# Four modulation vectors of a decoder layer: from ScalarE and GpSimd to VectorE, with new charges in a work-filling planner

## The chip, the cores and the metric

The kernel runs on one core of one Trainium2 chip. Its five engines are TensorE (PE in the profile, with PEld for its weight loads), VectorE (DVE), ScalarE (ACT), GpSimd (POOL) and SyncE (SP, which here only issues transfers). Each engine works through its own instructions in order. The metric is the device time of one execution in microseconds (us); lower is better.

## The reference, cut to what matters

One layer of a conditioned decoder for 1024 tokens of width 1024. A conditioning vector `c` gives six modulation vectors; two of them (shift 1, scale 1) are needed before anything else, the other four only later:

```
mod = silu(c) @ w_ada + b_ada          # 6 vectors of 1024: sh1, sc1, gt1, sh2, sc2, gt2
h   = rmsnorm(x, g_norm1) * (1 + sc1) + sh1
z   = h @ w_in                         # GLU pair | q | k | v | o | i | f | gate A | gate B
A   = silu(layernorm(dwconv31(glu_a * sigmoid(glu_b)))) @ w_conv_out
B   = mlstm_chunkwise(conv4(q), conv4(k), v, i, f) @ w_m_out
x   = x + gt1 * ((sigmoid(gA) * A + sigmoid(gB) * B) @ w_out)
h   = rmsnorm(x, g_norm2) * (1 + sc2) + sh2
out = rmsnorm(x + gt2 * hierarchical_moe(h), g_final)
```

## The kernel before, in words

Everything is float32. A matrix product is made of three products of rounded parts: a weight piece `raw` is split into a high part `wh` (cast on ACT, L150) and a low part `wl` (subtraction on DVE, L56), and the tokens are there as `hH` and `hL`.

The first half of the kernel is a list of PE jobs over the columns of `w_in` (`z_cols`, `z_tokens`, `z_tokens_wide`; the tiles `z` and `zt` are their sums). In order: the first GLU columns, the wide job (o columns and the i and f gates), the v columns, eight q and k jobs, two more o jobs, and sixteen jobs for the branch gates (A and B in turn, budget 7.5 each). PE works through the jobs one behind the other; the other engines' work is put between them by hand.

This is done by `fill(budget)`, called twice in a job. It takes one step of each of three queues of generators: `lat` (preparation of the mLSTM gates, then `mlstm()`, whose chunks pass through `step_a`, `step_b` and `step_c`), `lat2` (`conv_norm()`, which waits until `bulk` is empty) and `aux` (`ada_rest()`, later `clear_y()`, which writes zeros to `y_d`). What a step yields is its charge. The budget less the charges of `lat` and `lat2` is credit for `bulk`: the convolution of width 31, `conv31(m)` for four blocks of channels, one DVE operation a tap on 128x1024 elements (`cacc<-u,vec,cacc`, L64), charged 1.14. `aux` is stepped but not charged. So the tables of charges decide how many taps stand on DVE between two splits.

`ada_rest()` computes the four late vectors. Each has four blocks; a block is a transfer of 1 MB of `w_ada` into `ar` (two buffers, issued on SP behind the weight pieces `raw`) with two rows per partition. Before the change ACT multiplies each row by its element of silu(c) (L574), in place, and POOL adds it to `acc` (`tt(..., eng=G)`, L56; 28 additions in all). `column_sums` then sums `acc` over the partitions with PE (tile `modp`) and DVE writes `modc`.

When the jobs are done, `drain()` steps what is left of the queues: the mLSTM output is transposed (`psT`), scaled on ACT (`hs`, L903) and split (`bHt`, `bLt`), and the convolution result `cacc`, normed and through silu on ACT (L968), is split into `uH` (ACT) and `uL` (DVE). The first branch job (`yTrue`) needs all of `uH` and `uL`. After the branches come the product with `w_out`, routing, and the experts, whose weights fill the memory's bandwidth.

Of the kernel before, what the change touches and what calls it, by code (L numbers as in the profile page):

```python
# [12 lines left out]
AF = mybir.ActivationFunctionType  # L13
OP = mybir.AluOpType
# [4 lines left out]
P = 128  # L19
# [23 lines left out]
def hybrid_layer_kernel(ctx: ExitStack, tc: tile.TileContext, x, c, w_ada, b_ada, g_norm1, w_in, b_if,  # L43
# [9 lines left out]
    V, S, G, PE = nc.vector, nc.scalar, nc.gpsimd, nc.tensor  # L53

    def tt(o, a, b, op, eng=V):
        return eng.tensor_tensor(out=o, in0=a, in1=b, op=op)  # L56

    def ts(o, a, s1, op0, s2=None, op1=None, eng=V):
        if op1 is None:
            return eng.tensor_scalar(out=o, in0=a, scalar1=s1, scalar2=None, op0=op0)  # L60
        return eng.tensor_scalar(out=o, in0=a, scalar1=s1, scalar2=s2, op0=op0, op1=op1)

    def stt(o, a, s, b, op0, op1):
        return V.scalar_tensor_tensor(out=o, in0=a, scalar=s, in1=b, op0=op0, op1=op1)  # L64

    def mm(o, l, r, start, stop):
        return PE.matmul(o, l, r, start=start, stop=stop)  # L67
# [27 lines left out]
    silc = cst.tile([P, KT], F32, name="silc")  # L95
# [42 lines left out]
    def adab(vi, j, n):  # L138
        return vec[:, 64 + vi * KT + j:64 + vi * KT + j + n]
# [140 lines left out]
    lat, lat2, bulk, aux = [], [], [], []  # L280

    def step(q):
        while q:
            try:
                return next(q[0])
            except StopIteration:
                q.pop(0)
        return 0

    credit = [0.0]  # L290

    def fill(budget):

        credit[0] += budget - step(lat) - step(lat2)
        step(aux)
        while credit[0] > 0.5 and bulk:
            credit[0] -= step(bulk)
        if not bulk:
            credit[0] = 0.0
# [175 lines left out]
    def z_cols(c0, n, use, budget):  # L475

        W.add(w_in_k[:, :, c0:c0 + n], [P, KT, n])

        def job():
            wh, wl = W.take()  # L480
            ps = zps.tile([P, 2, 512], F32, tag="z", name=f"z{c0}")
            for k in range(KT):
                for j, (a, b) in enumerate(((wh, hH), (wh, hL), (wl, hH))):
                    for hf in range(2):
                        mm(ps[:n, hf, :], a[:, k, :], b[:, k, hf * 512:(hf + 1) * 512],
                           k == 0 and j == 0, k == KT - 1 and j == 2)
                if k == KT // 2 - 1:
                    fill(budget / 2)
            use(ps[:n].rearrange("p a b -> p (a b)"))
            fill(budget / 2)  # L490
        jobs.append(job)
# [55 lines left out]
    def ada_rest():  # L547
        raws = {}

        def load(i):  # L550
            vi = REST[i // 4]
            raws[i] = uo.tile([P, 2, D], F32, tag="ar", bufs=2, name=f"ar{i}")
            k = 2 * (i % 4)
            nc.sync.dma_start(raws[i], ada_v[:, k:k + 2, vi * D:(vi + 1) * D])

        def column_sums(n, acc):
            ps = mps.tile([P, 512], F32, tag="m", name=f"modp{n}")
            for j in range(KT):
                mm(ps[:, j:j + 1], acc[:, j * P:(j + 1) * P], ones[:, 0:1], True, True)
            tt(modc[:, n, :], ps[:, 0:KT], adab(REST[n], 0, KT), OP.add)  # L560

        load(0)
        yield 0
        pend = None
        for n in range(4):
            if pend:
                column_sums(*pend)
            acc = ml.tile([P, D], F32, tag="acc", bufs=1, name=f"acc{n}")
            for i in range(4 * n, 4 * n + 4):
                if i + 1 < 16:  # L570
                    load(i + 1)
                k = 2 * (i % 4)
                for q in range(2):
                    S.activation(raws[i][:, q, :], raws[i][:, q, :], AF.Copy, scale=silc[:, k + q:k + q + 1])  # L574
                if i % 4 == 0:
                    tt(acc, raws[i][:, 0, :], raws[i][:, 1, :], OP.add, eng=G)
                else:
                    for q in range(2):
                        tt(acc, acc, raws[i][:, q, :], OP.add, eng=G)
                yield 0  # L580
                yield 0
            pend = (n, acc)
        yield 0
        yield 0
        column_sums(*pend)
        yield 0
        yield 0
        yield 0
        ps = mps.tile([P, 512], F32, tag="m", name="modt")
        PE.transpose(ps[0:32, 0:P], modc.rearrange("p a b -> p (a b)"), ident)  # L590
        row = ml.tile([32, P], F32, name="modrow")
        S.copy(row, ps[0:32, 0:P])
        S.dma_start(mod_d[:, :], row)
# [181 lines left out]
    def hb(ap):  # L775
        return ap.unsqueeze(2).broadcast_to([P, NH, P])

    def mlstm():
# [30 lines left out]
        def step_b(cc):  # L809
            sl = slice(cc * P, (cc + 1) * P)  # L810
            PT, kw = held.pop(cc)
            vt = vts.pop(cc)
            psB = mps.tile([P, 3, P + 1], F32, tag="m", name=f"psB{cc}")

            def parts(i, name):
                t_ = mps.tile([P, 3, P + 1], F32, tag="m", name=f"{name}{cc}")
                return [t_[:, h, :] for h in range(3)] + [psB[:, i, :]]

            if cc > 0:
                psI = parts(0, "psI")  # L820
                for h in range(NH):
                    mm(psI[h], qT[h][:, sl], Cst[:, h, :], True, True)
            psN = parts(1, "psN")
            for h in range(NH):
                mm(psN[h], PT[:, h, :], vt[:, h, :], True, True)
            if cc + 1 < NT:
                psC = parts(2, "psC")
                for h in range(NH):
                    mm(psC[h], kw[:, h, :], vt[:, h, :], True, True)
                for h in range(NH):  # L830
                    if cc == 0:
                        V.tensor_copy(Cst[:, h, :], psC[h])
                    else:
                        stt(Cst[:, h, :], Cst[:, h, :], scl[:, cc, h:h + 1], psC[h], OP.mult, OP.add)
            num = ml.tile([P, NH, P + 1], F32, tag="num", name=f"num{cc}")
            den = ml.tile([P, NH], F32, tag="den", bufs=2, name=f"den{cc}")
            for h in range(NH):
                if cc > 0:
                    S.activation(num[:, h, :], psI[h], AF.Copy, scale=sint[:, cc, h:h + 1])
                    tt(num[:, h, :], num[:, h, :], psN[h], OP.add)  # L840
                else:
                    V.tensor_copy(num[:, h, :], psN[h])
            yield 4.0
            load_v(cc + 1)
            sos[cc] = ml.tile([P, NH, P], F32, tag="so", name=f"so{cc}")
            nc.sync.dma_start(sos[cc].rearrange("p h d -> p (h d)"), so_d[cc])
            hm = WT[cc]
            stt(den, num[:, :, P], -1.0, num[:, :, P], OP.mult, OP.max)
            tt(den, den, flo[:, cc, :], OP.max)
            V.reciprocal(den, den)  # L850
            tt(hm, num[:, :, 0:P], hb(den), OP.mult)
            bst = ml.tile([P, NH, 6], F32, tag="bst", bufs=2, name=f"bst{cc}")
            mv = ml.tile([P, NH, 2], F32, tag="mv", bufs=2, name=f"mv{cc}")
            lv = ml.tile([P, NH], F32, tag="lv", bufs=2, name=f"lv{cc}")
            for h in range(NH):
                V.bn_stats(out=bst[:, h, :], in_=hm[:, h, :])
            for h in range(NH):
                V.bn_aggr(out=mv[:, h, :], in_=bst[:, h, :])
            ts(lv, mv[:, :, 1], LN_EPS, OP.add)
            rsqrt(lv, lv, NH)  # L860
            held["n"] = (cc, mv, lv)
# [12 lines left out]
        for cc in range(NT):  # L874
            yield from step_b(cc)
            if cc + 1 < NT:
                step_a(cc + 1)
            yield 4.5
            step_c()
        yield 1.5  # L880
        while aux:
# [96 lines left out]
    for m in range(KT):  # L978
        for c0, dst in ((C_GA, sga_d), (C_GB, sgb_d)):
            def use(ps, c0=c0, m=m, dst=dst):  # L980
                sg = e4(f"g{c0}_{m}")
                S.activation(sg, ps, AF.Sigmoid)
                G.dma_start(dst[m], sg)
                if m == 0 and c0 == C_GA:
                    lat.append(mlstm())
                if m == 1 and c0 == C_GA:
                    lat2.append(conv_norm())
            z_cols(c0 + m * P, P, use, 7.5)


    bjobs = []
# [1115 lines left out]
```

## Time and profile before

| | us |
|---|---|
| median of 3 runs (1410.01 to 1417.47) | 1415.64 |
| the profiled execution | 1420.27 |
| its span, first to last instruction | 1418.5 |
| PE busy in it | 1305.4 (92%) |
| DVE busy | 986.0 (70%) |
| ACT busy | 515.2 (36%) |
| POOL busy | 311.9 (22%) |

Busy times are of the whole span. The page also cuts the span into 40 slices of some 35.5 us, with a digit for the busy tenths of each, and the clock that TensorE was granted, in tenths of full speed. The jobs over `w_in` end at about 581 us; from about 850 us on the transfers of expert weights are busy nearly all the time.

### The profile page before, as it was taken

The numbers are of one execution on the slowest core, as the hardware profiler recorded it, in microseconds if no ns is written. First come the engines' busy times: TensorE is split into PE (matmuls) and PEld (weight loads), VectorE is DVE, ScalarE is ACT, GpSimd is POOL, SyncE is SP. The second block draws the span as 40 slices with busy tenths as digits, with TensorE's granted clock in tenths as the row PEclk, the third lists the DMA queues.
The fourth block names the chain that finished last, engine by engine and source line by source line (L and its number), as shares of the span: only waits on it lengthen the run. The fifth ranks groups of instructions, "written<-read, shape, count | busy, mean of one in ns | idle before, by whom it ended". The sixth has DMA issues, their size and how long they took to land. (4 is left out here: it accounts for less than half of the span.)

```text
span 1418.5 us, 17679 instructions
## 1 busy us (share of the span) xinstructions
PE 1305.4 (92%) x6619; PEld 975.6 (69%) x6619; DVE 986.0 (70%) x1370; ACT 515.2 (36%) x685; POOL 311.9 (22%) x258
## 2 busy tenths in 40 slices
PE   3799888999999999999999689999999999998987
PEld 3578888879878888787888555666464756564643
DVE  5979998889976752556457776357575968585636
ACT  5232243323532224411232333235353735353523
POOL 2424355240421400105232102111010211110002
PEclk9899999999999999999999799999999999999999
DMA  8432434332453443454621449899999999999996
GB/s 280 138 119 94 174 121 148 107 112 80 148 171 124 145 140 107 143 182 148 197 90 74 182 179 381 322 360 404 412 410 405 410 381 415 391 413 387 404 352 264
DMA packets 121304, 337.50 MB, mean 238 GB/s; under 512 B 12532, under 2 KB 74272, under 8 KB 96384
## 3 DMA queue, kind: packets, MB, share of 16 engines
q1 hardware_dynamic: 106064, 290.81, 55.0%
q0 software_dynamic: 14672, 43.94, 8.2%
q10 hardware_dynamic: 480, 1.59, 0.3%
q8 instruction: 53, 0.87, 0.2%
q14 instruction: 35, 0.29, 0.1%
HBM read 303.37 MB, written 41.98 MB: 243 GB/s over the span
## 5 line engine op out<-in xcount | busy, mean ns | idle before, releaser
L56 DVE TENSOR_TENSOR wl<-big,wh 128x1024 fp32r<-128x1024 f32 x184 | 224.2, 1256 | 96.1 <-ACT wh L150 95.1
L150 ACT CAST wh<-big 128x1024 fp32r<-128x1024 f32 x184 | 185.8, 1049 | 156.1 <-DMA big<-in_w_e_gate_dram 83.0
L64 DVE SCALAR_TENSOR_TENSOR cacc<-u,vec,cacc 128x1024 f32<-128x1024 f32 x120 | 211.1, 1759 | 2.9
L67 PE MATMUL z<-hH,wh 128*128 128x512 f32 x512 | 168.6, 411 | 9.7 <-DVE hH L379 7.1
L67 PE MATMUL gu<-wh,tHLx 128*128 128x512 f32 x528 | 172.5, 408 | 2.3 <-ACT wh L150 1.1
L67 PE MATMUL z<-hL,wh 128*128 128x512 f32 x512 | 162.2, 398 | 0.2 <-POOL hL L56 0.2
L67 PE MATMUL z<-hH,wl 128*128 128x512 f32 x512 | 162.4, 399 | 0.0
L67 PE MATMUL gu<-big,tFx 128*64 128x512 f32 (+1 forms) x528 | 127.1, 617 | 0.0
L67 PEld LDWEIGHTS z<-hH,wh 128*128 128x128 f32 x512 | 97.3, 194 | 32.3 <-issue 8.7
L67 PEld LDWEIGHTS gu<-wh,tHLx 128*128 128x128 f32 x528 | 98.6, 192 | 28.9 <-ACT wh L150 6.6
L67 PEld LDWEIGHTS z<-hL,wh 128*128 128x128 f32 x512 | 97.7, 191 | 24.8 <-POOL hL L56 0.7
L67 PE MATMUL gu<-wl,tHLx 128*128 128x512 f32 x264 | 108.1, 409 | 6.9 <-DVE wl L56 6.9
L67 PEld LDWEIGHTS z<-hH,wl 128*128 128x128 f32 x512 | 97.8, 191 | 23.1
L1628 POOL DMA_INDIRECT y_d<-ye,idx x24 | 37.7, 1572 | 334.8 <-DVE ye L64 313.5
L56 DVE TENSOR_TENSOR wl<-raw,wh 128x1024 fp32r<-128x1024 f32 (+1 forms) x45 | 70.6, 1573 | 41.0 <-ACT wh L150 41.0
L67 PEld LDWEIGHTS gu<-big,tFx 128*64 128x64 f32 (+1 forms) x528 | 38.8, 142 | 70.9 <-issue 69.6
L56 POOL TENSOR_TENSOR acc<-acc,ar 128x1024 f32<-128x1024 f32 x24 | 71.1, 2961 | 59.8 <-ACT ar L574 50.8
L67 PE MATMUL zt<-wl,hH 128*128 128x256 f32 (+1 forms) x256 | 74.1, 289 | 5.2 <-DVE wl L56 5.2
L67 PE MATMUL zt<-wh,hH 128*128 128x256 f32 (+1 forms) x256 | 75.3, 294 | 1.3 <-ACT ev L634 1.2
L67 PE MATMUL zt<-wh,hL 128*128 128x256 f32 (+1 forms) x256 | 74.3, 290 | 0.0
L67 PE MATMUL py<-wh,tHLh 128*128 128x512 f32 x256 | 72.6, 404 | 0.5 <-DVE tHLx L56 0.4
L67 PE MATMUL o<-woH,mHL 128*128 128x512 f32 x256 | 72.9, 400 | 0.0
(419 smaller groups left out, 2164.9 us busy)
## 6 DMA issues: line engine op xcount, KB each, us to landing
big<-in_w_e_gate_dram SPq DMA_DIRECT2D x64, 1024.0 KB, 9.5
big<-in_w_e_up_dram SPq DMA_DIRECT2D x64, 1024.0 KB
big<-in_w_e_down_dram SPq DMA_DIRECT2D x64, 1024.0 KB, 9.5
raw<-in_w_in_dram SPq DMA_DIRECT2D x38, 512.0 KB, 4.3
ar<-in_w_ada_dram SPq DMA_DIRECT2D x16, 1024.0 KB, 6.2
araw<-in_w_ada_dram SPq DMA_DIRECT2D x8, 1024.0 KB, 10.1
y_d<-zero SPq DMA_DIRECT2D x16, 512.0 KB, 5.3
xall<-in_x_dram SPq DMA_DIRECT2D x8, 512.0 KB, 9.4
```

The costliest lines, as they stand in the source:

```text
L56: return eng.tensor_tensor(out=o, in0=a, in1=b, op=op)
L64: return V.scalar_tensor_tensor(out=o, in0=a, scalar=s, in1=b, op0=op0, op1=op1)
L67: return PE.matmul(o, l, r, start=start, stop=stop)
L150: S.copy(h, src)
L1628: G.indirect_dma_start(out=y_d[:, :], out_offset=bass.IndirectOffsetOnAxis(ap=idx[:, 1:2], axis=0), in_=src, in_offset=None, bounds_check= ...
```

## The change: what it does

In `ada_rest()` the eight rows of a vector are now taken up by DVE alone: the first by one `tensor_scalar` (`acc = row * silc`), each of the other seven by one `scalar_tensor_tensor` (`acc = row * silc + acc`). The 32 multiplications on ACT and the 28 additions on POOL are gone, 32 operations on DVE are new. There is one step to an operation, so two to a block as before, and each step is charged 0.6; `fill` now takes the charge of `aux` off the credit as well. In `mlstm()` the two charges of a chunk go from 4.0 and 4.5 to 3.4 each. The branch-gate jobs get a budget of 9.0 in place of 7.5.

```diff
     def fill(budget):
 
-        credit[0] += budget - step(lat) - step(lat2)
-        step(aux)
+        credit[0] += budget - step(lat) - step(lat2) - (step(aux) or 0)
         while credit[0] > 0.5 and bulk:
             credit[0] -= step(bulk)
...
                 k = 2 * (i % 4)
                 for q in range(2):
-                    S.activation(raws[i][:, q, :], raws[i][:, q, :], AF.Copy, scale=silc[:, k + q:k + q + 1])
-                if i % 4 == 0:
-                    tt(acc, raws[i][:, 0, :], raws[i][:, 1, :], OP.add, eng=G)
-                else:
-                    for q in range(2):
-                        tt(acc, acc, raws[i][:, q, :], OP.add, eng=G)
-                yield 0
-                yield 0
+                    if k + q == 0:
+                        ts(acc, raws[i][:, q, :], silc[:, 0:1], OP.mult)
+                    else:
+                        stt(acc, raws[i][:, q, :], silc[:, k + q:k + q + 1], acc, OP.mult, OP.add)
+                    yield 0.6
             pend = (n, acc)
...
-            yield 4.0
+            yield 3.4
             load_v(cc + 1)
...
-            yield 4.5
+            yield 3.4
             step_c()
...
-            z_cols(c0 + m * P, P, use, 7.5)
+            z_cols(c0 + m * P, P, use, 9.0)
```

On DVE, around the splits of the two pieces of the wide job (`wl` from `raw` 128x1056), this stood before:

```order
L56 TENSOR_TENSOR wl_852<-raw_715,wh_851 128x1056
L64 SCALAR_TENSOR_TENSOR cacc_626<-u_618,vec,cacc_626 128x1024 x7
L56 TENSOR_TENSOR wl_922<-raw_785,wh_921 128x1056
L56 TENSOR_TENSOR modc<-modp_952,vec 128x8
L64 SCALAR_TENSOR_TENSOR cacc_626<-u_618,vec,cacc_626 128x1024
```

and this stands there now:

```order
L56 TENSOR_TENSOR wl_844<-raw_713,wh_843 128x1056
L64 SCALAR_TENSOR_TENSOR acc_672<-ar_807,silc,acc_672 128x1024
L64 SCALAR_TENSOR_TENSOR cacc_626<-u_618,vec,cacc_626 128x1024 x3
L64 SCALAR_TENSOR_TENSOR acc_672<-ar_807,silc,acc_672 128x1024
L64 SCALAR_TENSOR_TENSOR cacc_626<-u_618,vec,cacc_626 128x1024 x2
L56 TENSOR_TENSOR wl_910<-raw_780,wh_909 128x1056
L56 TENSOR_TENSOR modc<-modp_940,vec 128x8
L60 TENSOR_SCALAR acc_950<-ar_874,silc 128x1024
```

Between the two splits seven taps have become five taps and two of the new operations.

Further on, at the start of the mLSTM (`PT` and `kw` are the first chunk's, `wl` the splits of branch-gate columns), DVE had before:

```order
L64 SCALAR_TENSOR_TENSOR cacc_2426<-u_997,vec,cacc_2426 128x1024 x7
L56 TENSOR_TENSOR wl_2824<-raw_2679,wh_2823 128x1024
L64 SCALAR_TENSOR_TENSOR cacc_2426<-u_997,vec,cacc_2426 128x1024
L56 TENSOR_TENSOR wl_2894<-raw_2752,wh_2893 128x1024
L56 TENSOR_TENSOR PT_2966<-psS_2961,WT_2485 128x512
L56 TENSOR_TENSOR kw_2973<-psK_2968,wk 128x512
L56 TENSOR_TENSOR wl_2977<-raw_2827,wh_2976 128x1024
```

and has now:

```order
L64 SCALAR_TENSOR_TENSOR cacc_2665<-u_981,vec,cacc_2665 128x1024 x7
L56 TENSOR_TENSOR wl_2856<-raw_2709,wh_2855 128x1024
L64 SCALAR_TENSOR_TENSOR cacc_2665<-u_981,vec,cacc_2665 128x1024 x4
L56 TENSOR_TENSOR PT_2931<-psS_2926,WT_2438 128x512
L56 TENSOR_TENSOR kw_2938<-psK_2933,wk 128x512
L64 SCALAR_TENSOR_TENSOR cacc_2665<-u_981,vec,cacc_2665 128x1024 x3
L56 TENSOR_TENSOR wl_2944<-raw_2785,wh_2943 128x1024
```

The last taps have moved behind the start of the mLSTM; from the last short convolution of a k block (`cv`) to `PT` there are 43 taps now and 30 before, with six splits and one first tap by `tensor_scalar` beside them in both.

At the end of the jobs ACT had before (`g` is a branch gate's sigmoid, `z_4228` the last job):

```order
L982 ACTIVATE g_7_4207<-z_4158 128x1024
L150 CAST uH_4219<-cacc_626 128x1024
L903 ACTIVATE hs_4258<-psT_4253,vec 128x128 x4
L150 CAST uH_4220<-cacc_969 128x1024
L982 ACTIVATE g_7_4292<-z_4228 128x1024
L903 ACTIVATE hs_4300<-psT_4295,vec 128x128 x4
L150 CAST uH_4221<-cacc_1535 128x1024
L903 ACTIVATE hs_4315<-psT_4310,vec 128x128 x4
L150 CAST uH_4222<-cacc_2426 128x1024
```

and has now (`z_4194` is the last job; three more pairs of `uH` and `hs` follow on the last row):

```order
L978 ACT_TABLE_LOAD
L978 ACTIVATE g_7_4256<-z_4194 128x1024
L899 ACTIVATE hs_4264<-psT_4259,vec 128x128 x4
L964 ACT_TABLE_LOAD
L964 ACTIVATE cacc_1957<-cacc_1957,vec 128x1024
L899 ACTIVATE hs_4277<-psT_4272,vec 128x128 x4
L964 ACTIVATE cacc_2665<-cacc_2665,vec 128x1024
L899 ACTIVATE hs_4290<-psT_4285,vec 128x128 x4
L150 CAST uH_4187<-cacc_626 128x1024
L899 ACTIVATE hs_4305<-psT_4300,vec 128x128 x4
```

Two of the four silus, two table loads and all four casts to `uH` now stand behind the last job's product.

## Rows read from the trace of the kernel before

**Rows 1.** Stretches: busy us by engine, PE, PEld, DVE, ACT, POOL; then granted clock.

```profile
142.00:337.00 195.00, 178.54 (x1036) 158.31 (x1036) 179.69 (x168) 63.47 (x68) 75.94 (x58) 0.96 0.38 132
415.00:421.00 6.00, 5.41 (x19) 4.41 (x20) 1.68 (x8) 0.00 (x0) 0.00 (x0) 0.50 0.72 238
```

**Rows 2.** Time line of PE: its waits from 75 to 581 us, in brackets.

```profile
152.29 0.59 PE L67 MATMUL zt<-wl,hH 128*128 128x264 f32 x1 [3.70 <-DVE wl L56]
177.04 0.39 PE L67 MATMUL zt<-wh,hH 128*128 128x256 f32 x1 [1.19 <-ACT ev L634]
190.70 0.39 PE L67 MATMUL zt<-wl,hH 128*128 128x256 f32 x1 [1.46 <-DVE wl L56]
199.97 3.58 PE L67 MATMUL modp<-ones,acc 128*128 128x1 f32 x16 [3.53 <-POOL acc L56]
226.50 0.40 PE L67 MATMUL psx<-dg,ones 32*128 32x32 f32 x2 [3.86 <-DVE dg L60]
311.79 0.95 PE L67 MATMUL z<-hH,wh 128*128 128x512 f32 x2 [2.62 <-ACT qk L661]
415.59 1.63 PE L67 MATMUL psN<-vt,PT 128*128 128x129 f32 x6 [3.00 <-DMA vt<-v_d]
```

**Rows 3.** Time lines of POOL and DVE, 130 to 163 us.

```profile
131.47 6.08 POOL L56 TENSOR_TENSOR acc<-acc,ar 128x1024 f32<-128x1024 f32 x2 [5.55 <-ACT ar L574]
130.64 8.00 DVE L64 SCALAR_TENSOR_TENSOR cacc<-u,vec,cacc 128x1024 f32<-128x1024 f32 x3
139.72 9.20 DVE L64 SCALAR_TENSOR_TENSOR cacc<-u,vec,cacc 128x1024 f32<-128x1024 f32 x7
161.76 1.22 DVE L56 TENSOR_TENSOR wl<-raw,wh 128x1024 fp32r<-128x1024 f32 x1
```

**Rows 4.** Groups of DVE instructions, 87 to 312 us: count | busy us, mean ns.

```profile
L64 DVE SCALAR_TENSOR_TENSOR cacc<-u,vec,cacc 128x1024 f32<-128x1024 f32 x81 | 148.5, 1833 | 1.9
L56 DVE TENSOR_TENSOR wl<-raw,wh 128x1024 fp32r<-128x1024 f32 (+1 forms) x17 | 31.7, 1877 | 5.5 <-ACT wh L150 5.5
L64 DVE SCALAR_TENSOR_TENSOR cv<-qk,vec,cv 128x1024 f32<-128x1024 f32 x12 | 15.4, 1285 | 0.4
```

**Rows 5.** The costliest group of POOL, 87 to 320 us.

```profile
L56 POOL TENSOR_TENSOR acc<-acc,ar 128x1024 f32<-128x1024 f32 x24 | 71.1, 2961 | 59.8 <-ACT ar L574 50.8 <-issue 7.8
```

**Rows 6.** The tile `ar`: its transfers, from issue to landing.

```profile
DMA to landing us min/median/max: 5.8/6.2/7.2
```

**Rows 7.** Time lines of PE, DVE, POOL and SP, 335 to 409 us.

```profile
335.76 0.63 PE L67 MATMUL z<-hH,wl 128*128 128x512 f32 x2
337.62 0.27 PE L590 MATMUL modt<-ident,modc 128*32 128x128 f32 x1
344.47 0.75 DVE L60 TENSOR_SCALAR cv<-qk,vec 128x1024 f32<-128x1024 f32 x1
358.67 4.66 POOL L56 TENSOR_TENSOR WT<-WT,negm 128x2048 f32<-128x2048 f32 x1
408.19 0.68 DVE L56 TENSOR_TENSOR PT<-psS,WT 128x512 f32<-128x512 f32 x1
408.76 0.73 SPq L791 DMA_DIRECT2D vt<-v_d  x1
```

**Rows 8.** Time lines of ACT and PE, 538 to 596 us.

```profile
538.24 1.28 ACT L968 ACT_TABLE_LOAD   x1
539.53 1.25 ACT L968 ACTIVATE cacc<-cacc,vec 128x1024 f32<-128x1024 f32 x1
581.46 1.02 ACT L982 ACTIVATE g<-z 128x1024 f32<-128x1024 f32 x1 [3.49 <-issue]
586.27 5.35 ACT L903 ACTIVATE hs<-psT,vec 128x128 f32<-128x128 f32 x20
595.29 0.63 PE L67 MATMUL yTrue<-uH,wh 128*128 128x512 f32 x2
```

## The prediction, made before the changed kernel ran

> **What bounds the kernel now.** I read the page first: PE is busy for 92% of the span, and after 850 us the transfers of expert weights fill the memory. The change touches neither stage, so what it can give must come from PE's idle time while the jobs over `w_in` run. The stretches show where that is. From 142 to 337 us PE is busy for 178.5 of 195 us, and its granted clock averages 0.96, although it has work queued all the time; DVE beside it is busy for 179.7 us [rows 1]. The reader should see two full engines, one of which stops now and then.
>
> The time line of PE names the stops. There are seven waits from 75 to 581 us, six of them before 337 us [rows 2]: two for `wl` and one for `dg`, which DVE writes, one for POOL's `acc`, one for `ev` and one for `qk` on ACT. The last two are DVE's as well: ACT's copies stood behind a silu or an `ev` that waited for DVE. The six add up to 3.70 + 1.19 + 1.46 + 3.53 + 3.86 + 2.62 = 16.4 us. After the longer ones the clock falls to its lower level, 1.2 GHz, for some us (0.50 from 415 to 421 us) [rows 1]; after the waits of 1.19 and 1.46 us it did not. A mean clock of 0.96 over 195 us is 195 x 0.04 = 7.8 us of work not done. So DVE being late costs this stretch 16.4 + 7.8 = 24.2 us.
>
> Why is DVE late? The time lines of POOL and DVE side by side show it. Seven taps with POOL idle take 9.20 us, 1.31 each; three taps while POOL makes two additions of together 6.08 us take 8.00 us, 4.1 more than 3 x 1.31 [rows 3]. While POOL adds, DVE gets hardly anything done. Over the whole stretch from 87 to 312 us, 81 taps have a mean of 1.833 us where the same operation with undisturbed neighbours (`cv`) has 1.285, and 17 splits have 1.877 where an undisturbed one takes 1.22 [rows 3, 4]. That is 81 x 0.548 + 17 x 0.66 = 55.6 us lost by DVE, about 2 us for each of the 28 additions, which take POOL some 3 us each (24 of them 71.1 us) [rows 5].
>
> **What is taken away.** The 28 additions on POOL go, and with them 55.6 us of DVE's stretch. The 32 multiplications on ACT go too; ACT was not late by its own work, so I count nothing for them.
>
> **What is added.** 32 operations on DVE of a tap's form and size: at most 32 x 1.285 = 41.1 us (the four first ones are cheaper). They are charged 32 x 0.6 = 19.2, which holds back 19.2 / 1.14 = 17 taps, 17 x 1.31 = 22.1 us, until later. DVE's load up to the last k jobs therefore changes by 41.1 - 55.6 - 22.1 = -36.6 us. It was late by at most a few us at each of PE's stops, so by this sum it arrives early at all six. Going through the new order with these durations from 84 us on, I get the second split of the wide job at about 140 us (PE wants it at 148.6), the next splits 4 us or more ahead, and `dg` nearly 3 us ahead. Bounds: none of the 24.2 us if DVE's loss has another cause than POOL, all of it otherwise. I take 24, since the time lines show the loss at the additions and nowhere else.
>
> **New waits on DVE for data.** The new operations read `ar` themselves, and whatever stands behind them waits too. A transfer lands 5.8 to 7.2 us after its issue [rows 6]. SP issues it right after the `raw` piece that waits for one split, and DVE needs it after the next split; between the two stand 10 to 12 us of DVE work in each block. So I cost it at nothing. The cover is about 4 us; without it every us late in each of 16 blocks would be up to 16 us on DVE.
>
> **The third sum over partitions.** Before, POOL finished `acc` ahead of PE's third `modp`. Now its last row stands on DVE behind the short convolution of the first q block: 0.2 + 1.0 (copy on ACT, a pass over the same size as the sigmoid in [rows 8]) + 0.75 + 3 x 1.285 (`cv`) + 1.285 = 7.1 us after that job's end. PE reaches `modp` half a job after it: eight products take 337.62 - 335.76 = 1.86 us [rows 7], so the 24 of half a job 5.6 us. A new wait of **1.5 us**, too short for the clock to fall by what the two shortest waits show. If it does, some 3 us.
>
> **The start of the mLSTM.** 13 more taps now stand ahead of `PT`. To check my way of adding, the order of before: from 337.62, where the last k job ends, `cv` starts 6.85 later (DVE is late) and takes 4.6; 30 taps in groups and a first tap are 39.4; six splits at 1.14 are 6.8; four POOL operations in that time cost DVE nearly their own length, 4.3 + 4.4 for `WT` (two; one of 4.66 is shown) and 4.2 for two channel sums. Sum 70.6; the trace has `PT` at 408.19, 70.6 after 337.62 [rows 7]. Now: `cv` starts 1.2 after the job's end, since DVE is no longer late, 4.6, then 43 taps and a first tap 56.2, splits 6.8, the two `WT` additions 8.7: 77.5, and `PT` is ready at 78.2. PE wants it for `psN` where it stopped before, at 415.59 - 3.00 = 412.6, which is 75.0 [rows 2]. So PE waits 3.2 us. Before, it waited 3.0 us there for `vt`, whose transfer SP issued only at 408.76, behind a `raw` piece that waited for a split [rows 7]; that split now comes at 62.6 and `vt` lands at about 70. One wait takes the place of the other, with the same drop of the clock after it: **+0.2 us**.
>
> **The end of the jobs.** The taps end later, so `conv_norm` starts three half jobs later, and more of its ACT work falls behind the last product. Before, the last gate's sigmoid starts at 581.46, and the first block of the branch product `yTrue` is through when the second starts at 595.29 [rows 8], 14 us after the last job. Now ACT has, from there: load 1.28, sigmoid 1.02, `hs` 1.07 (5.35 for five), load 1.28, silu 1.25, `hs`, silu 1.25, `hs`, then a cast to `uH` of about 1.0 [rows 8]; less 0.1 of overlap at each step, the first `uH` is there at some 10 us. The other three follow 2.0 us apart (`hs` between them), the last at 16; DVE's last `uL` is ready at 18 and the first `yTrue` block ends at 19. That is **+5 us**; bounds 2 (if the load runs ahead of the sigmoid's wait and DVE keeps up) and 8 (with a longer stretch at the lower clock).
>
> **The sum.** -24 + 1.5 + 0.2 + 5 = -17.3 us. What follows (branches, `w_out`, routing, experts) starts earlier by this and has the same instructions in the same order, so it shifts as a whole. The profiled execution of 1420.3 us would become 1403, its span 1401; it lies 4.6 us above the median of the runs, and from the median 1415.64 I get **1398 us**. A measurement of this kernel tells about 0.5%, 7 us, from no change.
>
> **Rivals.** *DVE becomes the bound (slower).* DVE was busy for 92% of 142 to 337 us [rows 1]. If its loss is not POOL's doing, DVE gets 41.1 - 22.1 = 19 us more to do there, its lateness passes the two jobs' cover of the splits, and PE waits for it: 1415.6 + 19 = 1435, more with the clock. It decides as soon as less than 19 of the 55.6 us come back. The Trainium skill speaks for it: "Perfetto Trace Analysis", section "Optimizing Scalar/DVE Operations", says that with a saturated DVE it can pay to move work to ScalarE or even GpSimd, the reverse of this change; by that sentence alone the result would be the 1435 above. The same place warns that a move between DVE and GpSimd may not help, as they share a port, and by that half the trace agrees: 8.00 us for three taps beside POOL, 3.9 without. Against this rival stand the rows: taps are long exactly where POOL adds. I give it 6%.
>
> *The gain is eaten by new waits.* The wait at `PT` grows (each us of DVE's lateness counts there), the third `modp` drops the clock, the end costs 8 us, and one or two of `ar`'s landings are late: -24 + 4.5 + 4 + 8 = -7.5, 1408, and worse with more of it. 20%, of which more than half would be no measurable change.
>
> *More than forecast.* DVE, freed, reaches `PT` in time, so the stop at 412.6 and the 3 us that its clock drop costs disappear, and the end costs only 2: -24 + 1.5 - 6 + 2 = -26.5, 1389. 12%.
>
> *The charges do nothing.* The order shows that taps did move, so only their effect could be nil; that lies within the cases above.
>
> **How the numbers follow.** The forecast has 62%, with a range of its own from 1391 to 1405. With the rivals: faster by over 0.5% (below 1408.6) 62 + 12 + 8 = 82%, within 0.5% 12%, slower 6%. The range that leaves out no more than two in ten goes from the rival with more gain to the one whose gain is nearly eaten: 1387 to 1411.
>
> **What would show it.** In the profile of the changed kernel: mean tap between 87 and 312 us near 1.3 us and no POOL additions there; no wait of PE for `wl`, `dg`, `ev` or `qk` between 142 and 330 us, and a granted clock of 0.98 or more in the counterpart of 142 to 337; a wait of 1 to 2 us at the third `modp`; PE waiting for `PT` and not for `vt` at the first `psN`; the last product of the jobs some 22 us earlier, the first `yTrue` block ending 19 us after it. I am wrong if taps stay at 1.8 us, if DVE shows idle time before `acc` for `ar`, or if PE's waits only move to other tiles.

## The result, and the profile after

The changed kernel takes 1402.24 us (median of 13 runs, 1397.82 to 1409.68) against 1415.64 of the kernel before (13 runs, 1407.94 to 1418.29): a ratio of 0.9918, 95% interval 0.9901 to 0.9935. The forecast was 1398. The profiled execution takes 1400.88 us with a span of 1399.1.

The stretches come first. The columns are, for each window: its length, busy time of PE, PEld, DVE, ACT and POOL with the number of instructions, PE's granted clock, the DMA share and GB/s.

```profile
142.00:317.00 175.00, 173.48 (x1046) 154.54 (x1045) 145.82 (x177) 42.22 (x47) 16.17 (x36) 0.98 0.41 137
236.00:244.00 8.00, 8.00 (x29) 6.75 (x30) 3.91 (x5) 1.83 (x2) 0.00 (x0) 0.57 0.49 161
241.00:243.00 2.00, 2.00 (x6) 1.52 (x6) 0.03 (x1) 0.00 (x0) 0.00 (x0) 0.50 1.10 362
395.00:401.00 6.00, 5.69 (x22) 5.30 (x23) 5.93 (x8) 0.00 (x0) 0.00 (x0) 0.54 0.01 2
```

The first window is the counterpart of 142 to 337 us in [rows 1]: nearly the same jobs, 20 us shorter. PE's idle time in it fell from 16.5 to 1.5 us, and DVE, which was busy for 92% of it, is now busy for 146 of 175 us. One stretch at the lower clock is left in it, after 236 us; the last row is the stretch behind PE's stop for `PT`.

The time line of PE has two waits from 75 us to the end of the jobs, where it had seven [rows 2]. The brackets give the idle time ahead of an instruction and what ended it.

```profile
235.61 2.58 PE L67 MATMUL modp<-ones,acc 128*128 128x1 f32 x16 [1.52 <-DVE acc L64]
395.31 1.63 PE L67 MATMUL psN<-vt,PT 128*128 128x129 f32 x6 [5.14 <-DVE PT L56]
```

The groups of DVE's instructions from 87 to 312 us (busy us, mean ns; then idle time ahead of them) answer to [rows 4]. Taps went from 1833 to 1282 ns and splits from 1877 (two wider ones counted in) to 1219; the new operations take 1275, and DVE is idle for nothing ahead of them, although `ar` lands 6.1 to 7.9 us after its issue, about as before [rows 6].

```profile
L64 DVE SCALAR_TENSOR_TENSOR cacc<-u,vec,cacc 128x1024 f32<-128x1024 f32 x72 | 92.3, 1282 | 1.4
L64 DVE SCALAR_TENSOR_TENSOR acc<-ar,silc,acc 128x1024 f32<-128x1024 f32 x28 | 35.7, 1275 | 0.0
L56 DVE TENSOR_TENSOR wl<-raw,wh 128x1024 fp32r<-128x1024 f32 x17 | 20.6, 1219 | 1.1 <-ACT wh L150 1.1
L60 DVE TENSOR_SCALAR acc<-ar,silc 128x1024 f32<-128x1024 f32 x4 | 3.0, 745 | 0.0
```

DVE's time line shows why PE stops at the third `modp` and at `PT`. The short convolution `cv` starts when the q job is copied; the last `acc` stands behind it and ends at 235.55, just when PE's `modp` starts. At 394 us four taps stand ahead of `PT`.

```profile
229.64 0.76 DVE L60 TENSOR_SCALAR cv<-qk,vec 128x1024 f32<-128x1024 f32 x1 [3.00 <-issue]
230.43 3.93 DVE L64 SCALAR_TENSOR_TENSOR cv<-qk,vec,cv 128x1024 f32<-128x1024 f32 x3
234.27 1.28 DVE L64 SCALAR_TENSOR_TENSOR acc<-ar,silc,acc 128x1024 f32<-128x1024 f32 x1
...
335.55 6.41 DVE L64 SCALAR_TENSOR_TENSOR cacc<-u,vec,cacc 128x1024 f32<-128x1024 f32 x1
...
352.25 4.99 DVE L61 TENSOR_SCALAR cacc<-u,vec 128x1024 f32<-128x1024 f32 x1
...
389.37 5.24 DVE L64 SCALAR_TENSOR_TENSOR cacc<-u,vec,cacc 128x1024 f32<-128x1024 f32 x4
394.53 0.68 DVE L56 TENSOR_TENSOR PT<-psS,WT 128x512 f32<-128x512 f32 x1
```

The 6.41 and 4.99 us are one operation each, held up beside the two additions for `WT` that POOL still makes:

```profile
336.24 4.63 POOL L56 TENSOR_TENSOR WT<-WT,negm 128x2048 f32<-128x2048 f32 x1
...
351.57 5.12 POOL L56 TENSOR_TENSOR WT<-WT,negm 128x2048 f32<-128x2048 f32 x1
```

At the end of the jobs PE is through with its last product and starts `psT` at 560.72, and ACT goes through the chain that the prediction lists. Before, the gate's sigmoid, the last `hs` and two of the four casts to `uH` stood behind the last job; now two silus of the convolution (L964), two table loads and all four casts stand there.

```profile
560.95 1.28 ACT L978 ACT_TABLE_LOAD   x1 [3.29 <-issue]
562.24 1.02 ACT L978 ACTIVATE g<-z 128x1024 f32<-128x1024 f32 x1
563.16 1.13 ACT L899 ACTIVATE hs<-psT,vec 128x128 f32<-128x128 f32 x4
564.32 1.28 ACT L964 ACT_TABLE_LOAD   x1
565.61 1.24 ACT L964 ACTIVATE cacc<-cacc,vec 128x1024 f32<-128x1024 f32 x1
...
569.88 1.08 ACT L150 CAST uH<-cacc 128x1024 fp32r<-128x1024 f32 x1
...
575.72 1.18 ACT L150 CAST uH<-cacc 128x1024 fp32r<-128x1024 f32 x1
```

```profile
579.00 0.74 PE L67 MATMUL yTrue<-uL,wh 128*128 128x512 f32 x2 [0.55 <-DVE uL L56]
...
580.05 0.63 PE L67 MATMUL yTrue<-uH,wh 128*128 128x512 f32 x2
```

The second block of `yTrue` starts at 580.05, 19.3 us after 560.72.

### The profile page after: what moved, and what is told of

The parts are those of the page before. It is cut to its first block, busy times and chain, and to the rows that moved or that the text cites. A ratio compares the mean times of both kernels' runs of the same rounds, so it can differ in the third digit from the quotient of the medians.

```text
span 1399.1 us, 17600 instructions
## 1 busy us (share of the span) xinstructions
PE 1296.0 (93%) x6619; PEld 965.0 (69%) x6619; DVE 968.9 (69%) x1402; ACT 477.7 (34%) x650; POOL 230.1 (16%) x230
## 5 line engine op out<-in xcount | busy, mean ns | idle before, releaser
L64 DVE SCALAR_TENSOR_TENSOR cacc<-u,vec,cacc 128x1024 f32<-128x1024 f32 x120 | 159.1, 1326 | 2.8
L67 PEld LDWEIGHTS gu<-wl,tHLx 128*128 128x128 f32 x264 | 50.0, 189 | 27.6 <-DVE wl L56 16.9
L56 DVE TENSOR_TENSOR wl<-raw,wh 128x1024 fp32r<-128x1024 f32 (+1 forms) x45 | 57.1, 1274 | 15.7 <-ACT wh L150 15.7
```

## The experiments

All kernels were timed beside the kernel before. Since timed medians of one kernel differ by some us from chip to chip, each is also read by a length within its profile that holds all the jobs and nothing of the experts: from the last group of `pada` products (about 71 us) to the first `yFalse` product. It is 561.45 us in the kernel before (72.90 to 634.35) and 548.52 in the changed one (70.93 to 619.45).

| kernel | ratio to before | 95% interval | `pada` to `yFalse`, us |
|---|---|---|---|
| before | 1 | | 561.45 |
| changed | 0.9918 | 0.9901 to 0.9935 | 548.52 |
| operations alone, two runs | 0.983 and 0.9888 | 0.9793 to 0.9868; 0.9863 to 0.9914 | 543.17 and 540.81 |
| charges alone | 0.9963 | 0.9942 to 0.9983 | 555.39 |
| multiplications left on ACT | 1.0015 | 0.9991 to 1.0039 | 561.87 |
| changed, 28 POOL additions back | 1.0140 | 1.0106 to 1.0173 | 579.70 |
| changed, POOL memsets instead | 0.9941 | 0.9923 to 0.9960 | 548.84 |
| changed, last two rows in one step | 0.9882 | 0.9857 to 0.9907 | 542.36 |
| operations alone, last two rows in one step, two runs | 0.9851 and 0.9835 | 0.9820 to 0.9882; 0.9807 to 0.9863 | 534.33 and 538.56 |
| charge of the late vectors alone | 1.0060 | 1.0038 to 1.0081 | 567.07 |
| chunk and gate charges alone | 0.9864 | 0.9831 to 0.9898 | 543.28 |
| last two rows in one step, 0.2 a step | 0.9799 | 0.9775 to 0.9824 | 533.13 |

**The operations without the new charges.** The change's `ada_rest()` with `fill`, chunk steps and gate budget as before:

```diff
-        credit[0] += budget - step(lat) - step(lat2) - (step(aux) or 0)
+        credit[0] += budget - step(lat) - step(lat2)
+        step(aux)
...
-                    yield 0.6
+                    yield 0
...
-            z_cols(c0 + m * P, P, use, 9.0)
+            z_cols(c0 + m * P, P, use, 7.5)
```

> The new operations alone, with the old charges: taps stand where they stood before, the 32 operations are added. If DVE's time lost beside POOL is the cause, DVE's load from 87 to 312 us is 41.1 - 55.6 = -14.5 us of before's, the six old waits of PE go or nearly go, but the sums over partitions wait longer (2 to 6 us with the clock), PT is ready early, and the first branch block ends 14 us after the last job as before: 1393 to 1401, as fast as the whole change or faster. If the gain came from holding taps back (the charges), this is 1410 to 1418.

The median is 1392.33 us, faster than the whole change. All six early waits are gone here too; the tail is nearly the old one (14.8 us from the last job to the second block of `yTrue`, against 14.07 before and 19.3 in the changed kernel); PE doesn't stop at `psN`; and there are two waits for `acc`:

```profile
190.14 2.08 PE L67 MATMUL modp<-ones,acc 128*128 128x1 f32 x9 [2.73 <-DVE acc L64]
243.42 2.61 PE L67 MATMUL modp<-ones,acc 128*128 128x1 f32 x16 [1.52 <-DVE acc L64]
```

So the operations by themselves give all of the gain. By the length within the profile (543.17 and 540.81 against 548.52) the charges take 5 to 8 us of it back; of the two timed ratios one lies clear of the changed kernel's interval and the other overlaps it.

**The charges without the operations.** The old `ada_rest()`, with `yield 0.6` in both of its steps, and the new charges elsewhere.

> The new charges alone, with ACT's multiplications and POOL's additions as before: 17 taps, 22 us, are held back, DVE's loss beside POOL stays. If lateness of DVE by whatever means is the cause, most of the six waits shrink, the wait at PT and the later end (some 5 us) come: 1402 to 1410. If only POOL's removal counts, no gain: 1415 to 1422.

1408.86 us, as expected. Taps stay long, and yet four of the six early waits are gone, since fewer taps stand ahead of the splits; two are left, and the one at `psN`:

```profile
165.20 0.39 PE L67 MATMUL zt<-wh,hH 128*128 128x264 f32 x1 [2.05 <-ACT ev L633]
212.52 0.40 PE L67 MATMUL psx<-dg,ones 32*128 32x32 f32 x2 [2.90 <-DVE dg L60]
403.05 1.63 PE L67 MATMUL psN<-vt,PT 128*128 128x129 f32 x6 [8.86 <-DVE PT L56]
```

```profile
L64 DVE SCALAR_TENSOR_TENSOR cacc<-u,vec,cacc 128x1024 f32<-128x1024 f32 x69 | 127.7, 1850 | 1.5
```

The price is visible at `PT`: 8.86 us. Operations and charges cure the same lateness of DVE, so what they give doesn't add up: 18 to 21 us and 6 us apart, 13 together.

**The multiplications left on ACT.** DVE only adds; everything else is the changed kernel:

```diff
+                    S.activation(raws[i][:, q, :], raws[i][:, q, :], AF.Copy, scale=silc[:, k + q:k + q + 1])
...
-                        ts(acc, raws[i][:, q, :], silc[:, 0:1], OP.mult)
+                        V.tensor_copy(acc, raws[i][:, q, :])
...
-                        stt(acc, raws[i][:, q, :], silc[:, k + q:k + q + 1], acc, OP.mult, OP.add)
+                        tt(acc, acc, raws[i][:, q, :], OP.add)
```

> The whole change, but ACT multiplies as before and DVE only adds (the same number of DVE operations of the same size). If ACT's relief is worth nothing, as predicted, 1401 to 1407 (some us may be lost where an addition on DVE waits for ACT behind a silu). If ACT's 35 us were what made PE wait, 1410 or more.

1417.3 us: no gain at all, and my expectation of 1401 to 1407 missed. DVE was relieved of POOL here as well (taps take 1283 ns), but its additions stood idle for 25.6 us from 87 to 312 us, all of it for ACT's product. The time lines of ACT and of DVE show how: ACT's product stands behind a step of the gates (`lz`, `lu`) that waits for DVE, and DVE's addition waits for that product.

```profile
182.32 0.23 ACT L683 ACTIVATE lz<-lz 128x32 f32<-128x32 f32 x1 [4.32 <-DVE lz L64]
182.46 1.14 ACT L573 ACTIVATE ar<-ar,silc 128x1024 f32<-128x1024 f32 x1
183.61 1.28 ACT L690 ACT_TABLE_LOAD   x1
189.03 0.23 ACT L690 ACTIVATE lu<-lu 128x32 f32<-128x32 f32 x1 [4.13 <-DVE ld L60]
```

```profile
182.10 0.19 DVE L64 SCALAR_TENSOR_TENSOR lz<-ifc 128x32 f32<-128x32 f32 x1
183.62 1.23 DVE L56 TENSOR_TENSOR acc<-acc,ar 128x1024 f32<-128x1024 f32 x1 [1.34 <-ACT ar L573]
```

PE then waits 4.76 us at the second `modp` and 5.16 at the third. The time alone would also fit the other reading that I had put down, that ACT's own work made PE wait. The trace speaks against it: ACT is busy for 66 of the 195 us from 142 to 337. The gain was lost because DVE's additions hang on ACT's place in the order.

**POOL's additions put back as ballast.** Beside each accumulating operation POOL adds a row to a scratch tile that nothing reads:

```diff
+        scr = ml.tile([P, 896], F32, name="scr")
+        G.memset(scr, 0.0)
...
                         stt(acc, raws[i][:, q, :], silc[:, k + q:k + q + 1], acc, OP.mult, OP.add)
+                        tt(scr, scr, raws[i][:, q, 0:896], OP.add, eng=G)
```

> The whole change, and beside it 28 additions on POOL into a scratch tile of 896 columns whose result nobody uses. If POOL's additions are what holds DVE up, a tap beside one is again about 2 us longer, DVE's load grows by about 50 us and PE's waits come back: 1415 to 1430. If the gain came from ACT or from the charges, as the changed kernel: 1400 to 1405.

1435.53 us, just above the 1415 to 1430 that I had expected. Groups of DVE and of POOL from 87 to 312 us:

```profile
L64 DVE SCALAR_TENSOR_TENSOR cacc<-u,vec,cacc 128x1024 f32<-128x1024 f32 x63 | 114.1, 1811 | 1.4
```

```profile
L56 POOL TENSOR_TENSOR scr<-scr,ar 128x896 f32<-128x896 f32 x26 | 68.9, 2648 | 84.2 <-DMA ar<-in_w_ada_dram 83.4
```

Taps are back at 1.81 us, and so are the waits: 7.41 us at the first `modp`, 4.36 for a `wl`, 2.50 for `dg`, 7.56 at the third `modp`. DVE's loss by POOL is shown, and with the additions of the change on top of it the kernel is slower than before: this is the rival of a bound DVE, come true where POOL is not relieved.

**POOL kept as busy, reading only a column.** To tell whether any work on POOL does this or only that form:

```diff
                         stt(acc, raws[i][:, q, :], silc[:, k + q:k + q + 1], acc, OP.mult, OP.add)
+                        G.tensor_copy(scr[:, 0:1], raws[i][:, q, 0:1])
+                        for _ in range(3):
+                            G.memset(scr, 0.0)
```

> The whole change, and for each of its 28 accumulating operations one copy of a column and three memsets of 128x896 on POOL, about 2.6 us, as long as the additions put back in an earlier run (2.64 us each, which made the kernel 33 us slower with taps of 1.81 us). They add nothing to the result. Theory A (any long operation on POOL holds DVE up): taps at 1.6 to 1.9 us, 1425 to 1440 us. Theory B (it is the form, two inputs read and one written, that collides): taps at 1.28 us, 1400 to 1405 us.

1407.23 us, a little above the expected 1400 to 1405, but its interval overlaps the changed kernel's, and the profile's length is 548.84 against 548.52 without the memsets. The same two groups:

```profile
L64 DVE SCALAR_TENSOR_TENSOR cacc<-u,vec,cacc 128x1024 f32<-128x1024 f32 x71 | 91.0, 1282 | 1.4
```

```profile
L581 POOL MEMSET scr<- 128x896 f32 x81 | 69.1, 853 | 4.7
```

69.1 us of memsets leave taps at 1282 ns, 68.9 us of additions make them 1811. So it is not POOL's being busy that holds the taps up, but its additions, which read two tiles while DVE's tap reads two as well; the memsets read none. That the reading is the reason was not separated further by a run. The Trainium skill, "SBUF — State Buffer", section "Who interferes with whom", states this: a VectorE instruction with two inputs in SBUF contends with a GpSimd instruction that reads SBUF, not with one that only writes. By that rule the memsets cost the taps nothing and the additions much, and both runs agree. One other form did feel POOL here: the first operation of `cv`, with one input, took 1033 ns on the mean over seven, against 755 in the changed kernel.

**The last two rows of a vector in one step.** `acc` is ready half a job earlier, so PE should not wait at `modp`. First on the changed kernel:

```diff
-                    yield 0.6
+                    if k + q < 6:
+                        yield 0.6
+                if k == 6:
+                    yield 1.2
+                    yield 0
```

> The whole change with the last two rows of each vector in one step. Theory: the third modp wait goes with its clock drop, 1.5 + 3.4 = 4.9 us, 1397 us; the wait of 5.1 us for PT and the tail of 19 us stay as they are. Rival (DVE is late as such): no gain, 1400 to 1403.

1397.84 us. The wait at `modp` is gone, the one for `PT` (5.14 us) and the tail are as in the changed kernel, and the length fell by 548.52 - 542.36 = 6.2 us, where 4.9 were expected. The rival (DVE late as such, no gain) falls by the length; the timed intervals still overlap. Then on the operations alone, with `yield 0` in both places:

> The operations of the change with the old charges, and the last two rows of each vector taken in one step, half a job earlier, so that acc is finished ahead of PE's modp. Theory (the two waits for acc, 2.73 and 1.52 us in the trace of the operations alone, cost their length and a stretch of about 20 us at a mean clock of 0.83 each, 3.4 us of work): 2.7 + 1.5 + 3.4 + 3.4 = 11 us less than the operations alone, 1381 us, no wait for modp and no clock below 0.98 from 100 to 340 us. Rival (DVE, busy for 19.7 of 20 us there, is simply late, and the wait moves to the next split): at most 4 us less, 1388 or more, with waits for wl in place of those for acc.

The 1381 us that I expected were missed, with 1392.56. The length fell from 543.17 to 534.33 and the `modp` waits are gone; but waits for `lf` (1.13 us) and `dg` (2.75 us) came in, so that the rival, a wait that moves, was in part right. The timed ratio was no better than that of the operations alone on another chip, so both were run again side by side:

> The same kernel as the one with the old charges and the last two rows in one step, beside the operations alone and on the same chip, since its profile was 9 us shorter up to the second branch product (534.3 against 543.2 us from the last product before the jobs) and its timed runs were not. Theory (the 9 us are real and the runs of two chips can't be compared): a ratio of 0.976 to 0.980, some 8 us below the operations alone. Rival (the later stages give them back): no difference between the two.

> The operations of the change with the old charges once more, as the measure for the first two kernels on the same chip: ratio 0.982 to 0.985, waits of 2.7 and 1.5 us for acc again.

1391.13 against 1395.79 us: some 5 us where I had expected 8, with intervals that just touch, so that a gain by this step on the operations alone is likely and not shown by the times. Both ratios (0.9835 and 0.9888) came out higher than I had expected. The two profiles of the kernel with the rows in one step have the same waits and lengths of 534.33 and 538.56: the clock makes most of the difference, as the last section shows.

**The charges one by one.** Only the 0.6 a step of the late vectors:

> Of the new charges only the 0.6 a step of the late vectors; chunk steps 4.0 and 4.5, gate budget 7.5 as before. The order has 39 taps ahead of PT (43 in the whole change, 30 before), and the last tap stands eleven splits behind PT (four in the whole change, two before). Theory: PT comes 5 us earlier than in the whole change and PE waits little there, but the norm of the convolution starts seven jobs later and falls behind the last job: 1410 to 1430 us, slower than the whole change. Rival (the tail is only the silu's chain and doesn't care when the taps end): 1394 to 1398.

1422.59 us, slower than before, as expected. PE doesn't stop at `psN`, with 39 taps ahead of `PT` where the changed kernel has 43. The last product of the jobs ends early (at 547.7 us), but the norm of the convolution is not done:

```profile
552.14 2.07 PE L67 MATMUL meanb<-csum,ones 128*128 128x512 f32 x2 [3.52 <-POOL csum L56]
573.04 3.15 PE L67 MATMUL psv<-ones,csq 128*128 128x1 f32 x14 [14.11 <-POOL csq L56]
580.58 3.78 PE L67 MATMUL rvb<-dgrv,ones 128*128 128x128 f32 x16 [3.97 <-POOL dgrv L56]
591.43 1.22 PE L67 MATMUL yTrue<-uH,wh 128*128 128x512 f32 x2 [7.06 <-ACT uH L150]
```

From the last job to `yFalse` it takes 90.3 us where the changed kernel takes 58.6. And the chunk and gate charges without the 0.6 (the edit of `fill` and `yield` of the first experiment alone):

> The whole change without the 0.6 a step of the late vectors. The order has 30 taps ahead of PT and two splits behind it, as with the old charges. Theory (the 10 us between the whole change and its operations alone come from the 0.6 a step, by way of PT and the tail): 1390 to 1395 us, no wait for PT, last job to second branch block 14 us. Rival (the chunk charges or the gate budget cost it): 1398 to 1403.

1395.35 us, 543.28 in the profile: the same as the operations alone, with the same two `modp` waits (2.75 and 1.52). So the chunk and gate charges neither cost nor give anything by themselves. Together with the 0.6 they bring back most of what it pushes behind the last job, and they move more taps ahead of `PT`: the stop of 5.14 us there is in neither of these two kernels and needs both kinds of charge.

**A third of the charge.** The rows in one step, the new chunk and gate charges, and 0.2 in place of 0.6 (0.4 for the last two rows):

> The whole change with the last two rows in one step and 0.2 a step in place of 0.6. The order has 5 taps fewer ahead of dg than with no charge, 36 taps ahead of PT (43 in the whole change) and two splits behind it. Theory (PE waits only where DVE is late by a few us, and 9 more taps fit ahead of PT): no wait for dg, lf, modp or PT, the tail as before the change, 4 us of waits and some 2 of clock less than with the old charges: 528 us from the last product before the jobs to yFalse, 6 us below it in time. Rival (the 0.6 is what costs, in proportion): PE waits 1 us or more for PT and the tail is 2 us longer, no gain on it.

1383.74 us, a ratio of 0.9799, faster than the changed kernel and the lowest median in this study. From 142 to 317 us PE never stops and its clock never falls:

```profile
142.00:317.00 175.00, 175.00 (x1084) 156.85 (x1083) 161.62 (x190) 42.22 (x47) 15.39 (x36) 1.00 0.42 142
```

```profile
388.74 0.91 PE L67 MATMUL psN<-vt,PT 128*128 128x129 f32 x6 [2.65 <-DMA vt<-v_d]
```

One expectation failed: at `psN` PE waits 2.65 us, but for `vt`, as in the kernel before [rows 2], not for `PT`. SP issued it at 383.22, behind a `raw` piece at 382.75, and PE had it 5.5 us later. I had expected 528 us to `yFalse`; it is 533.13.

## Why the prediction was right, and where it was not

**The mechanism held.** DVE was late because POOL's additions held it up: with them gone taps and splits take their undisturbed times (1282 and 1219 ns), with them back taps take 1811, with memsets of the same length 1282. The six waits and their clock, -24.2, went as forecast; what remains of lost clock from 142 to 317 us is 175 x 0.02 = 3.5 us, and that is the new `modp` stretch. `ar` cost nothing, as reckoned.

**"The third sum over partitions" was mis-sized.** The wait is 1.52 us, as forecast (1.5). But the prediction called it "too short for the clock to fall by what the two shortest waits show". It fell, to a mean of 0.57 over 8 us, 3.4 us of work: 4.9 in all, and taking the wait away gave 6.2. The rows that I argued from, two waits of 1.19 and 1.46 us, were too few to carry "too short". The second price that the prediction named, "some 3 us" if the clock falls, is the 3.4 that came.

**"The start of the mLSTM" was mis-sized by 2 us.** From the end of the last k job (315.19) to `psN` it takes 80.1 us where it took 415.59 - 337.62 = 78.0 [rows 2, 7]: +2.1 for a forecast of +0.2. `PT` started at 79.3 instead of 77.5. The two `WT` additions cost 6.41 - 1.28 and 4.99 - 0.8 = 9.3 us where I had put 8.7. Of the other 1.2 us, 0.4 is DVE's wait for `wh` ahead of the split at 324.15, and some 0.6 the 43 taps, which follow each other at 1.30 us (9.12 for seven) where I had taken 1.285:

```profile
324.15 1.23 DVE L56 TENSOR_TENSOR wl<-raw,wh 128x1024 fp32r<-128x1024 f32 x1 [0.40 <-ACT wh L150]
325.29 9.21 DVE L64 SCALAR_TENSOR_TENSOR cacc<-u,vec,cacc 128x1024 f32<-128x1024 f32 x7
334.41 1.22 DVE L56 TENSOR_TENSOR wl<-raw,wh 128x1024 fp32r<-128x1024 f32 x1
```

**"The end of the jobs" held.** 19.3 us for a forecast of 19, and 14.07 before: +5.3. The operations alone, whose taps end where they ended before, have nearly the old tail (14.8), so it is the charges' doing.

**The sum.** -24.2 + 4.9 + 2.1 + 5.3 = -11.9; the length within the profile gives 548.52 - 561.45 = -12.9, the medians -13.4, the forecast -17.3. The us between -11.9 and -12.9 lies in the first term: from the `pada` products to the end of the last k job it takes 244.3 us where it took 264.7, 20.5 less, and -24.2 + 4.9 makes 19.3. The last product of the jobs comes 18.5 us earlier by this measure, where the prediction named some 22. The profiled executions differ by more, 1400.88 - 1420.27 = -19.4: 2.0 of it lie ahead of the jobs and 4.5 behind `yFalse` (784.2 and 779.7 us to the end), where nothing was changed and where profiles of this study lie between 775 and 786. That the profiled execution came out close to the 1403 of the prediction, and even below it, is luck.

**What the prediction did not see** is a step under "What is added". It took -36.6 us for DVE's load as one sum, of which -22.1 came from the charge, and never asked whether -14.5, the operations alone, would do. They do: the charges buy only the second `modp` wait (2.73 us and its clock), and cost 5.14 us and a clock drop at `PT` and the tail's 5. That is why the operations alone are 5 to 8 us shorter in the profile. The rival "gain eaten by new waits" was therefore half true, though not by the landings of `ar`; "more than forecast" shows what was left to get, and the last experiment got it. The first rival, DVE as the bound, is what the kernel with POOL's additions back does.

Whether ACT's 32 multiplications cost anything in the arrangement of before, with POOL adding, was not tried by itself; I had counted nothing. Their going does not carry the gain alone: the kernel with POOL's additions back has them gone too, and its waits are back.

## What to carry to other kernels

Before counting an engine's busy time as load, look for operations that are longer than the same form elsewhere, and at which engine's work they lie beside: here 55 us of DVE's load were POOL's, and with 32 operations more DVE is busy for 968.9 us of the span where it was busy for 986.0. What two edits give that relieve the same lateness doesn't add up, so price each alone; the second may only move work to where the next wait is. A queue's charge is a lever with two ends: what it takes away from the front it puts in front of the next consumer, here `PT`, and of the tail.

## What the runs showed of the hardware

The same program with the same waits had its clock fall in one execution and not in the other. The kernel of the operations with the last rows in one step waited 2.75 us for `dg` in both of its profiles. Its two stretches from 210 to 220 us:

```profile
210.00:220.00 10.00, 9.23 (x77) 9.18 (x78) 8.71 (x33) 2.78 (x6) 1.50 (x3) 1.00 0.37 135
```

```profile
210.00:220.00 10.00, 9.70 (x58) 9.63 (x59) 8.28 (x28) 0.52 (x1) 0.00 (x0) 0.67 0.35 130
```

The first ran at full clock throughout, the second at a mean of 0.67, 3.3 us of work in ten. So the length of this wait did not decide whether the clock falls, and a term of some 3 us behind it is a chance and not a sum. At the third `modp` it was no chance: in all five profiles with the 1.52 us wait there, and in the one with 1.92 us (the memsets), the clock fell to 0.50, while behind the 2.65 us ahead of `psN` in the last experiment it stayed at 1.00. Behind the wait at `modp` stand 16 small products that took 2.58 us in the changed kernel, and behind the two short waits of the kernel before stood the products of a job; whether that makes the difference was not tried. The other thing is POOL's form: memsets of 853 ns beside the taps cost them nothing, while 26 additions of 2.65 us cost DVE 63 x (1.811 - 1.282) = 33 us on the taps alone.
